# Second layer's ffn: its first four feature tiles by eight plain products instead of seven

## The chip, the cores and the metric

The kernel runs on one core of one Trainium2 chip. The metric is the device time of one execution in microseconds; runs of the same kernel differ by about 0.05%. Every number below is from one profiled execution and from the times of three more runs.

## The reference: what is computed

The kernel is one inference step of a two-layer trunk over 128 context tokens and 512 latent tokens, held side by side as 642 columns (two of them padding). Each layer is: normalise and modulate, attention, output projection and residual, normalise and modulate, a convolutional ffn and residual. The change lies in the second layer's ffn:

```python
def conv_ffn(h, w_up, conv_w, conv_b, w_down):
    u = h @ w_up                                  # 1024 -> 2 * 2816
    up = jnp.pad(u, ((0, 0), (pad, pad), (0, 0)))
    u = sum(up[:, j:j + n] * conv_w[j] for j in range(CONV_W)) + conv_b    # three taps along the tokens
    a, gt = u[..., :D_FF], u[..., D_FF:]
    return (jax.nn.silu(gt) * a) @ w_down
```

## The kernel before

Features lie on partitions and tokens along the free dimension. The ffn's 2816 features are 22 **tiles** of 128; each has an a side and a g side. The 642 columns are two **halves** of 322 and 320, and the 1024 input features two groups of four 128-row blocks (q = 0 to 3). So one tile is a 2 × 2 block product: weights A11, A12 (a side) and A21, A22 (g side) times the normalised rows B11, B21 (first half) and B12, B22 (second half).

Every matmul is done with numbers split into an upper part (a cast, `hi`) and a lower part (`lo` = number minus cast), three matmuls for each 128 × 128 block: hi·hi, hi·lo, lo·hi. A block product over four blocks q is 12 matmuls of 322 columns. A split is a cast on ScalarE (line 117) and a subtraction on VectorE or GpSimd (line 113); for weights it is made by `block`, which goes from the raw tile (`raw`, DMA of 512 KB) to a ring of ten pairs `w2`.

Seven products do for eight (Strassen's scheme in Winograd's form): with weight sums S1 to S4 (`sums`, on GpSimd) and row sums T1 to T4 (on VectorE), the products are A11·B11, A12·B21, S4·B22, A22·T4, S1·T1, S2·T2, S3·T3 (`p1` to `p7`), 84 matmuls, and `u2`, `u3`, `c22`, `c21`, `c12` add them up from PSUM on VectorE into `ca` and `cg` (line 1930). Products take PSUM tiles `p` from a ring of six, in the order in which they are made.

A tile's convolution is `gid` (ScalarE: centre tap of g into the only PSUM tile `v`), `tapg` (two VectorE steps), `silu` (ScalarE), `aid` (ScalarE: centre of a, again into `v`), `tapa`, `mul` (VectorE, into `va`), `ghi` (ScalarE cast) and `glo` (VectorE). Then four tiles at a time go through the down product (`down`), which adds to the residual `x`.

`begin` makes the second half of the attention's output projection (for each of eight column blocks j: `product`, then the residual addition `add_x` on VectorE and a square on ScalarE) and, between its blocks, the normalised first half. Its list `after` says what is issued behind each block. From line 1741 on `begin` makes tiles 0 and 1 while the second half's normalised rows and T1 to T4 come into being. `middle` makes tiles 2 and 3 (`lead`), then every tile from 4 on is one `slot` with down products of the chunk before it woven in. All engines keep the order in which the program issues; the compiler moves nothing here.

In the second half the row factor `rs1` needs the squares of all eight blocks (three small matmuls on TensorE, `rs_sum`); before the change the parts of the T sums that don't need it are made ahead of it: `scaled` and `steps` (into `second`), `shifts` (into `c1` and `first`, with the difference of shifts `ds`).

Of the kernel before, what the change touches and what calls it, by code (L numbers as in the profile page):

```python
# [1527 lines left out]
class Mix:  # L1528
# [105 lines left out]
    def begin(self, po, oT, xsrc):  # L1634
        nc, t, V, G, n, l = self.nc, self.t, self.V, self.G, range(self.KP), self.l
# [21 lines left out]
        halves = lambda tag, m: [self.T(po, tag, [P, HB], F32, m) for _ in range(m)]  # L1657
        first = [self.pair(po, "first", 4) for _ in n]
        second = [self.pair(po, "second", 4) for _ in n]
        c1, rr = halves("c1", 4), halves("rs", 3)  # L1660
        tile = lambda: self.T(po, "sq", [P, HB], F32, 3)
        ht = [[self.T(self.pm, "ht", [P, 3, HB], F32R, 8) for _ in range(2)] for _ in n]
# [41 lines left out]
        def scaled(q):  # L1704
            for v, c in self.groups(1):
                V.tensor_scalar(out=second[q][:, 0, c], in0=self.x[q][:, HB:][:, c], scalar1=mod[:, 4, q, v : v + 1], scalar2=None, op0=ALU.mult)

        def steps(q):
            for v, c in self.groups(1):
                V.scalar_tensor_tensor(out=second[q][:, 1, c], in0=self.x[q + 4][:, HB:][:, c], scalar=mod[:, 4, q + 4, v : v + 1],  # L1710
                                       in1=second[q][:, 0, c], op0=ALU.mult, op1=ALU.subtract)

        def shifts(q):
            b = first[q][:, 0]
            for v, c in self.groups(1):
                nc.scalar.activation(c1[q][:, c], b[:, c], AF.Identity, scale=-1.0, bias=mod[:, 3, q, v : v + 1])
            for v, c in self.groups(1):
                V.tensor_scalar(out=b[:, c], in0=b[:, c], scalar1=ds[:, q, v : v + 1], scalar2=None, op0=ALU.add)
# [22 lines left out]
        self.p1(0)  # L1741
        scaled(0), steps(0)
        block("S2", 0, V), block("S3", 0, V)
        self.copy1(0)
        rs1 = self.rs_of(sqs1, 1, rr[1], rr[2])
        self.p2(0), self.p1(1)
        shifts(0)
        self.copy1(1), self.copy2(0)
        self.p1(2), self.p2(1)
        qs = (3, 1, 2, 0)  # L1750

        def lows(name, q, src):
            t.low(self.rows[name, q][1], src, self.rows[name, q][0])

        def pieces(name, src, store, make, between=()):

            between, last = deque(between), None
            for q in qs:
                make(q)
                self.rows[name, q] = store(q)  # L1760
                nc.scalar.copy(self.rows[name, q][0], src(q))  # L1761
                if last is not None:
                    lows(name, last, src(last))
                if between:
                    between.popleft()()
                last = q
            lows(name, last, src(last))
            for step in between:
                step()

        row = lambda m: lambda q: [h[:, m] for h in ht[q]]
        wide = lambda q: self.act(1)
        one, two = lambda q: first[q][:, 0], lambda q: first[q][:, 1]
        three, four = lambda q: second[q][:, 0], lambda q: second[q][:, 1]

        def t2(q):
            V.tensor_mul(four(q), four(q), rs1)
            V.tensor_add(one(q), four(q), one(q))

        def t3(q):  # L1780
            for v, c in self.groups(1):
                nc.scalar.activation(four(q)[:, c], four(q)[:, c], AF.Identity, bias=ds[:, q, v : v + 1])

        def t1(q):
            V.tensor_mul(three(q), three(q), rs1)
            V.tensor_add(three(q), three(q), c1[q])

        pieces("T2", one, row(0), t2, [lambda: (self.copy2(1), self.copy1(2)), lambda: (self.p1(3), self.p2(2)),
                                       lambda: (self.copy1(3), self.copy2(2)), lambda: (self.p2(3), self.copy2(3))])
        s1 = self.T(po, "s1", [P, D])  # L1790
        self.sums(1, 0, s1)
# [36 lines left out]
    def lead(self, f, pv, nx):  # L1828
# [8 lines left out]
        if nx == self.LEAD:  # L1837
            block("A11")
# [452 lines left out]
```

## Time and profile before

| | us |
|---|---|
| three runs: median, lowest, highest | 1750.52, 1750.12, 1750.91 |
| the profiled execution: its own time, its span | 1746.39, 1744.5 |
| busy in the span: TensorE, VectorE, ScalarE, GpSimd | 1590.6, 1285.3, 928.4, 800.1 |

A busy TensorE is not one at its peak: matmuls are pipelined, and a matmul that is issued late or at the slower clock counts as busy too. Idle time of the other engines costs nothing where TensorE does not wait for them.

### The profile page before, as it was taken

What the parts mean: (1) busy time and instruction counts of PE and PEld (TensorE: products, weight loads), DVE (VectorE), ACT (ScalarE), POOL (GpSimd) and SP (SyncE); (2) the same over time, 40 slices, a digit from 0 to 9 for tenths busy, and PEclk for the clock granted to TensorE, in tenths of its full rate; (3) what the DMA queues carried; (4) which work ended last, traced back from release to release, by engine and by line L of the source; (5) the groups of instructions that cost most, each with busy time, mean ns of one, the idle gap of its engine ahead of it and who ended that gap; (6) DMA issues with size and microseconds to landing.
All of it is one profiled execution on the core that took longest, in us unless ns stands there. A gap on an engine that the chain in (4) does not pass through costs nothing.

```text
span 1744.5 us, 28162 instructions
## 1 busy us (share of the span) xinstructions
PE 1590.6 (91%) x10301; PEld 1512.9 (87%) x10301; DVE 1285.3 (74%) x2226; ACT 928.4 (53%) x1788; POOL 800.1 (46%) x769
## 2 busy tenths in 40 slices
PE   8878888888998999999988999979768999999996
PEld 2867877788898999999988999969757999999996
DVE  4895888778888779877458677774877667776765
ACT  3555777644554345534355778783444344444444
POOL 2164777462252534252171445563327456555532
PEclk9999999999999999999999999989888999999998
DMA  8440121062444444453144111114212222222311
GB/s 334 134 134 26 53 67 61 13 223 82 128 138 145 159 141 147 134 165 120 58 133 153 41 56 51 44 61 142 79 60 73 78 86 87 76 76 77 96 47 61
DMA packets 79176, 176.14 MB, mean 101 GB/s; under 512 B 11614, under 2 KB 29358, under 8 KB 79038
## 3 DMA queue, kind: packets, MB, share of 16 engines
q1 hardware_dynamic: 76542, 170.08, 30.4%
q10 hardware_dynamic: 2304, 4.20, 0.7%
q8 instruction: 81, 1.33, 0.3%
q14 instruction: 57, 0.47, 0.1%
q0 software_dynamic: 192, 0.07, 0.0%
HBM read 167.24 MB, written 8.03 MB: 100 GB/s over the span
## 4 chain that ended last, share of the span: by engine, by line
PE 55%; DVE 13%; ACT 5%; issue 4%; DMA 3%; POOL 1%; SPq 0%; DVEq 0%; ACTq 0%; POOLq 0%
PE mm L137 25%; PE p L1579 24%; DMA mraw<-in_w_mod_dram 3%; DVE acc L316 1%; PE sc L1202 1%; PE tr L1240 1%; DVE wlo L113 1%; PE o L1252 1%; DVE v L1966 1%; ACT w L117 1%; ACT whi L117 0%; DVE pt L113 0%; DVE u L505 0%; DVE nt L424 0%; DVE ha L438 0%
## 5 line engine op out<-in xcount | busy, mean ns | idle before, releaser
L314 POOL TENSOR_TENSOR acc<-acc,mt 128x512 f32<-128x512 f32 x115 | 178.7, 1554 | 262.3 <-ACT mt L313 259.4
L137 PE MATMUL mm<-ha,whi 128*128 128x352 f32 (+1 forms) x1168 | 287.3, 328 | 8.2 <-DVE u L507 3.7
L137 PE MATMUL mm<-hb,whi 128*128 128x290 f32 (+1 forms) x1168 | 245.2, 303 | 2.8 <-ACT hb L437 1.9
L137 PEld LDWEIGHTS mm<-ha,whi 128*128 128x128 f32 (+1 forms) x1168 | 202.8, 190 | 10.6 <-issue 3.8
L316 DVE SCALAR_TENSOR_TENSOR acc<-mraw,cs,acc 128x512 f32<-128x512 f32 (+1 forms) x165 | 164.9, 1006 | 53.9 <-DMA mraw<-in_w_mod_dram 50.8
L137 PEld LDWEIGHTS mm<-hb,whi 128*128 128x128 f32 (+1 forms) x1168 | 193.6, 192 | 5.3 <-issue 3.0
L137 PE MATMUL mm<-ha,wlo 128*128 128x352 f32 (+1 forms) x584 | 189.3, 324 | 0.0
L113 POOL TENSOR_TENSOR wlo<-raw,whi 128x1024 fp32r<-128x1024 f32 (+3 forms) x45 | 95.7, 2132 | 177.3 <-ACT whi L117 107.8
L137 PE MATMUL mm<-hb,wlo 128*128 128x290 f32 (+1 forms) x584 | 175.3, 300 | 0.0
L137 PE MATMUL mm<-g,whi 128*128 128x352 f32 (+1 forms) x704 | 157.5, 311 | 6.5 <-DVE x L447 5.2
L117 ACT CAST whi<-raw 128x1024 fp32r<-128x1024 f32 (+3 forms) x115 | 113.8, 995 | 69.0 <-PE mm L137 52.5
L113 POOL TENSOR_TENSOR w<-raw,w 128x512 fp32r<-128x512 f32 (+1 forms) x65 | 86.9, 1345 | 135.7 <-ACT w L117 132.3
L1579 PE MATMUL p<-g,d 128*128 128x320 f32 (+1 forms) x912 | 141.9, 314 | 4.4 <-ACT d L117 2.6
L313 ACT ACTIVATE mt<-mraw,cs 128x512 f32<-128x512 f32 x115 | 81.9, 720 | 116.6 <-DMA mraw<-in_w_mod_dram 103.7
L1579 PEld LDWEIGHTS p<-g,d 128*128 128x128 f32 x912 | 137.9, 191 | 6.4 <-ACT d L117 2.8
L1579 PE MATMUL p<-ht,w 128*128 128x322 f32 x792 | 130.6, 320 | 10.9 <-ACT ht L1761 4.8
L1579 PEld LDWEIGHTS p<-ht,w 128*128 128x128 f32 x792 | 123.8, 195 | 12.7 <-ACT ht L1761 5.4
L1579 PE MATMUL p<-hb,w 128*128 128x322 f32 (+1 forms) x696 | 115.3, 319 | 13.7 <-DVE cg L1930 7.8
L137 PEld LDWEIGHTS mm<-g,whi 128*128 128x128 f32 x704 | 118.3, 189 | 8.6 <-ACT ha L437 3.8
L1579 PEld LDWEIGHTS p<-hb,w 128*128 128x128 f32 x696 | 108.6, 196 | 15.3 <-ACT w L117 4.2
L1579 PE MATMUL p<-ha,w 128*128 128x322 f32 x696 | 113.5, 318 | 0.6 <-ACT ca L1924 0.5
L137 PEld LDWEIGHTS mm<-hb,wlo 128*128 128x128 f32 (+1 forms) x584 | 113.1, 194 | 0.2 <-issue 0.2
(339 smaller groups left out, 3835.9 us busy)
## 6 DMA issues: line engine op xcount, KB each, us to landing
raw<-in_w_up_dram SPq DMA_DIRECT2D x92, 512.0 KB, 3.6
mraw<-in_w_mod_dram SPq DMA_DIRECT2D x128, 256.0 KB, 2.9
raw<-in_w_out_dram SPq DMA_DIRECT2D x18, 512.0 KB, 4.0
raw<-in_w_in_odd_dram SPq DMA_DIRECT2D x18, 512.0 KB, 3.5
mraw<-in_w_mod_dram SPq DMA_DIRECT2D x16, 512.0 KB, 8.8
raw<-in_w_down_dram SPq DMA_DIRECT2D x16, 512.0 KB, 3.6
draw<-in_w_down_dram SPq DMA_DIRECT2D x40, 192.0 KB, 2.5
raw<-in_w_down_dram SPq DMA_DIRECT2D x16, 384.0 KB, 3.1
```

Source lines behind the costliest of these rows:

```text
L113: (engine or self.nc.vector).tensor_sub(lo, src, Fv(hi))
L117: self.nc.scalar.copy(hi, src)
L137: self.pe = self.nc.tensor.matmul(out, lhsT=l, rhs=r, start=k == 0, stop=k == n - 1)
L313: nc.scalar.activation(t, raw, AF.Copy, scale=s)
L314: nc.gpsimd.tensor_add(acc, acc, t)
L316: nc.vector.scalar_tensor_tensor(out=acc, in0=raw, scalar=s, in1=acc, op0=ALU.mult, op1=ALU.add)
L1202: nc.tensor.matmul(ps[:, c : c + n], lhsT=u.Q[:, a], rhs=x[e], start=e == 0, stop=e == 1)
L1240: nc.tensor.transpose(tp[:, j * P : (j + 1) * P], u.p[b][:, x : x + P], self.ident)
L1252: nc.tensor.matmul(u.o[:, u.t[c][2]], lhsT=v, rhs=u.t[c][e], start=c == 0 and e == 0, stop=c == 4 and e == 1)
L1579: self.t.pe = self.nc.tensor.matmul(ps[:, 0:n], lhsT=l_, rhs=r[:, 0:n], start=first and m == 0, stop=last and m == count - 1, skip_group_c ...
L1966: self.V.scalar_tensor_tensor(out=v[:, d], in0=self.flat(c)[:, s], scalar=self.t.convw[:, self.l, j, n : n + 1], in1=v[:, d], op0=ALU.mult ...
```

## The change

Tiles 0 to 3 are made by eight plain products, half by half. `plain(f, side, half)` makes both block products of one side and half into one PSUM tile (24 matmuls), and `copy` takes it to `ca` or `cg` on ScalarE. The order of TensorE is then: first halves of tiles 0, 1, 2; second halves of 2, 1, 0; tile 3, whose second half is begun with twelve matmuls of either side (products 13 and 14) and ended after its first half. I number these products 1 to 18. The second half's rows are normalised as the first half's are (`scale1`, `shift1`), and T1 to T4 (`sums_t`, `uppers`, `lowers`) are made from them during products 7 to 14, for tile 4, which is the first by seven products. Tile 0's weights are loaded and split a second time. The rings of `ca` and `cg` become 3 and 3 instead of 4 and 2.

```diff
         after = {
-            2: lambda: (self.blocks_a(0, V), self.load("a", 3), norm0(3, 4)),
-            3: lambda: (self.blocks_a(1, G), self.load("a", 0), norm0(5, 6)),
-            4: lambda: (self.blocks_a(2, G), self.load("g", 0), norm0(7), scaled(3), lower0(7), steps(3)),
-            5: lambda: (self.blocks_a(3, V), self.load("a", 1), shifts(3), scaled(1), steps(1)),
-            6: lambda: (self.sums(0, 0), shifts(1), scaled(2), steps(2)),
-            7: lambda: (self.sums(0, 1), self.load("g", 1), shifts(2)),
+            2: lambda: (self.blocks_of(0, "a", V), self.load("g", 1), norm0(3, 4)),
+            3: lambda: (self.blocks_of(0, "g", G), self.load("a", 2), norm0(5, 6)),
+            4: lambda: (self.blocks_of(1, "a", G), self.load("g", 2), norm0(7), lower0(7)),
+            5: lambda: (self.blocks_of(1, "g", G), self.load("a", 0)),
+            6: lambda: (self.blocks_of(2, "a", V), self.load("g", 0)),
+            7: lambda: None,
...
+        self.plain(0, 0, 0)
         rs1 = self.rs_of(sqs1, 1, rr[1], rr[2])
...
+        self.plain(0, 1, 0)
+        self.blocks_of(2, "g", G)
+        for k in (0, 1):
+            scale1(k), shift1(k)
+        self.copy(0, 0, 0)
+        for n, (f, side) in enumerate(((1, 0), (1, 1), (2, 0), (2, 1))):
+            self.plain(f, side, 0)
+            if n < 3:
+                for k in (2 * n + 2, 2 * n + 3):
+                    scale1(k), lower1(k - 2), shift1(k)
+            self.copy(*((0, 1), (1, 0), (1, 1), (2, 0))[n], 0)
+        lower1(6), lower1(7)
+        self.blocks_of(0, "a", G)
+
+        self.plain(2, 0, 1)
+        sums_t(0), uppers(0)
+        self.copy(2, 1, 0)
+        self.load("a", 3)
+        self.plain(2, 1, 1)
+        sums_t(1), lowers(0)
+        self.copy(2, 0, 1), uppers(1)
+        self.plain(1, 0, 1)
+        sums_t(2), lowers(1)
+        self.copy(2, 1, 1), self.gid(2), uppers(2)
+        self.blocks_of(0, "g", G), self.load("g", 3)
+        self.plain(1, 1, 1)
+        sums_t(3), self.tapg(2), lowers(2)
+        self.copy(1, 0, 1), self.silu(2), self.aid(2), uppers(3)
+        self.blocks_of(3, "g", G)
+        self.load("a", 4)
+        self.plain(0, 0, 1)
+        self.tapa(2), lowers(3)
+        self.copy(1, 1, 1)
+        self.blocks_of(3, "a", G)
+        self.load("g", 4)
+        self.plain(0, 1, 1)
+        self.copy(0, 0, 1)
+
+        self.plain(3, 1, 1, 0), self.plain(3, 0, 1, 0)
+        self.copy(0, 1, 1)
+        for q in n_:
+            upper("T1", q, source["T1"](q), self.act(1))
+            if q:
+                lower("T1", q - 1, source["T1"](q - 1))
+        lower("T1", 3, source["T1"](3))
 
     def middle(self):
+        block = lambda *names: [self.block(name, 4) for name in names]
+        tag = lambda f, *names: [getattr(self, name)(f) for name in names]
+        tag(2, "mul", "ghi")
+        self.sums(4, 0)
+        self.plain(3, 0, 0)
+        tag(1, "gid", "tapg"), tag(2, "glo"), tag(1, "silu", "aid")
+        block("A11"), self.sums(4, 1)
+        self.plain(3, 1, 0)
+        tag(1, "tapa", "mul"), block("S2")
+        tag(0, "gid"), tag(1, "ghi"), block("S3")
...
+        tag(0, "tapg"), tag(1, "glo"), tag(0, "silu", "aid"), block("S1")
...
+        tag(0, "tapa"), block("A12"), self.load("a", 5)
+        tag(0, "mul", "ghi"), block("A22")
+        self.copy(3, 1, 1), self.gid(3)
+        tag(0, "glo"), block("S4"), self.load("g", 5)
...
+    def plain(self, f, side, half, kk=None):
+        names = (("A11", "A12"), ("A21", "A22"))[side]
+        for k in (0, 1) if kk is None else (kk,):
+            key = "C", f, side, half
+            if key not in self.p:
+                self.p[key] = self.t.PS("p")
+            w = self.blocks[names[k], f]
+            row = (("B11", "B21"), ("B12", "B22"))[half][k]
+            self.matmuls(self.p[key], HB, [(self.columns(w, q), self.rows[row, q]) for q in range(self.KP)], k == 0, k == 1)
+
+    def copy(self, f, side, half):
+        c = (self.ca, self.cg)[side][f]
+        self.nc.scalar.copy(c[:, half], self.p.pop(("C", f, side, half))[:, 0:HB])
+        if half:
+            self.pads(c)
```

Three places of the order show what moves. The first is VectorE at the end of the output projection, from the residual addition of one column block (`x_2560` before, `x_2556` after) to that of the last (`x_2556` before, `x_2552` after). Before:

```order
L1590 SCALAR_TENSOR_TENSOR x_2560_13195<-p_2682_13833,mod1_83,x_2560_13195 128x190
L1590 SCALAR_TENSOR_TENSOR x_2560_13195<-p_2682_13833,mod1_83,x_2560_13195 128x128
L1601 TENSOR_TENSOR sq_2676_13812<-sq_2667_13761,sq_2676_13812 128x322
L1718 TENSOR_SCALAR first_2533_13161<-first_2533_13161,ds_2622_13523 128x190
L1718 TENSOR_SCALAR first_2533_13161<-first_2533_13161,ds_2622_13523 128x132
L1706 TENSOR_SCALAR second_2538_13166<-x_2560_13195,mod1_83 128x190
L1706 TENSOR_SCALAR second_2538_13166<-x_2560_13195,mod1_83 128x132
L1710 SCALAR_TENSOR_TENSOR second_2538_13166<-x_2587_13300,mod1_83,second_2538_13166 128x190
L1710 SCALAR_TENSOR_TENSOR second_2538_13166<-x_2587_13300,mod1_83,second_2538_13166 128x132
L1590 SCALAR_TENSOR_TENSOR x_2556_13185<-p_2685_13874,mod1_83,x_2556_13185 128x190
L1590 SCALAR_TENSOR_TENSOR x_2556_13185<-p_2685_13874,mod1_83,x_2556_13185 128x128
```

After:

```order
L1591 SCALAR_TENSOR_TENSOR x_2556_13191<-p_2677_13815,mod1_83,x_2556_13191 128x190
L1591 SCALAR_TENSOR_TENSOR x_2556_13191<-p_2677_13815,mod1_83,x_2556_13191 128x128
L1602 TENSOR_TENSOR sq_2671_13802<-sq_2662_13755,sq_2671_13802 128x322
L113 TENSOR_TENSOR w2_2680_13846<-raw_2656_13714,w2_2679_13845 128x512
L113 TENSOR_TENSOR w2_2682_13850<-raw_2656_13714,w2_2681_13849 128x512
L1591 SCALAR_TENSOR_TENSOR x_2552_13181<-p_2684_13855,mod1_83,x_2552_13181 128x190
L1591 SCALAR_TENSOR_TENSOR x_2552_13181<-p_2684_13855,mod1_83,x_2552_13181 128x128
L1617 TENSOR_TENSOR rs_2542_13170<-rs_2541_13169 128x322
```

Between the two additions stood two steps each of `shifts` (L1718), `scaled` (L1706) and `steps` (L1710); now two weight splits (tile 2's a side) stand there, and the first step of the row factor follows at once.

The second is VectorE where the lower parts of T1 (`hb`) end. Before, the last ones and what follows them:

```order
L1785 TENSOR_TENSOR second_2536_13164<-second_2536_13164,rs_2545_13173 128x322
L1786 TENSOR_TENSOR second_2536_13164<-second_2536_13164,c1_2540_13168 128x322
L113 TENSOR_TENSOR hb_2726_14182<-second_2538_13166,hb_2725_14181 128x322
L1930 TENSOR_TENSOR cg_2729_14191<-p_2720_14154,ca_2697_13978 128x322
L113 TENSOR_TENSOR hb_2728_14188<-second_2536_13164,hb_2727_14187 128x322
L113 TENSOR_TENSOR w2_2731_14195<-s1_2702_14066,w2_2730_14194 128x512
```

After:

```order
L113 TENSOR_TENSOR hb_2750_14406<-first_2532_13160,hb_2749_14405 128x322
L113 TENSOR_TENSOR hb_2752_14409<-first_2533_13161,hb_2751_14408 128x322
L113 TENSOR_TENSOR hb_2754_14413<-first_2534_13162,hb_2753_14412 128x322
L113 TENSOR_TENSOR hb_2756_14417<-first_2535_13163,hb_2755_14416 128x322
L1992 TENSOR_TENSOR va_2757_14425<-v_2734_14293,cg_2687_13885 128x642
L1969 SCALAR_TENSOR_TENSOR v_2762_14458<-cg_2689_13887,convw_434,v_2762_14458 128x641 x2
L113 TENSOR_TENSOR g_2759_14428<-va_2757_14425,g_2758_14427 128x642
L113 TENSOR_TENSOR w2_2765_14467<-raw_2739_14306,w2_2764_14466 128x512
L1969 SCALAR_TENSOR_TENSOR v_2763_14464<-ca_2688_13886,convw_434,v_2763_14464 128x641 x2
L1992 TENSOR_TENSOR va_2768_14500<-v_2763_14464,cg_2689_13887 128x642
L113 TENSOR_TENSOR w2_2770_14503<-s_2760_14430,w2_2769_14502 128x512
```

Before, additions from PSUM and a weight split follow T1, and the first convolution comes later. Now tile 2's `mul` (`va_2757`), then tile 1's taps on g (`v_2762`), tile 2's `glo`, a weight split, tile 1's taps on a (`v_2763`) and its `mul` stand behind them.

The third is ScalarE around the centre tap that follows tile 0's (after) or tile 2's (before) `ghi`, the cast into `g`. Before, with `v_2811` the centre of tile 3's g side:

```order
L1993 CAST g_2804_14558<-va_2803_14556 128x642
L117 CAST w2_2807_14574<-raw_2787_14468 128x512
L117 CAST w2_2809_14578<-s_2794_14510 128x512
L1960 ACTIVATE v_2811_14584<-cg_2799_14534,convb_436,convw_434 128x642
L117 CAST w2_2812_14587<-raw_2786_14466 128x512
L117 CAST w2_2816_14607<-raw_2787_14468 128x512
L117 CAST w2_2818_14613<-s4_2798_14531 128x512
L117 CAST w2_2824_14637<-raw_2814_14591 128x512
L1978 ACTIVATE cg_2799_14534<-v_2811_14584 128x642
```

After, with `v_2789` the centre of tile 3's g side:

```order
L1996 CAST g_2785_14565<-va_2784_14563 128x642
L117 CAST w2_2787_14568<-raw_2745_14348 128x512
L1854 COPY cg_2777_14516<-p_2747_14377 128x322
L1963 ACTIVATE v_2789_14574<-cg_2777_14516,convb_436,convw_434 128x642
L117 CAST w2_2790_14577<-s4_2766_14470 128x512
L117 CAST w2_2797_14603<-raw_2783_14561 128x512
L1981 ACTIVATE cg_2777_14516<-v_2789_14574 128x642
L1927 COPY ca_2799_14610<-p_2795_14587 128x322
```

Now a copy from PSUM, `cg_2777` from `p_2747` (product 13, closed as product 18), stands behind the `ghi` and a weight cast; before there was no copy from PSUM in this place.

## Rows read from the trace of the kernel before

**Rows 1.** Busy us by engine (instructions), granted clock (PEclk), DMA share, by stretch.
```profile
1235.80:1351.30 115.50, 81.90 (x429) 75.86 (x428) 85.07 (x148) 53.68 (x106) 52.20 (x47) 0.84 0.20 63
...
1352.00:1452.00 100.00, 99.97 (x672) 99.70 (x671) 69.59 (x118) 42.40 (x74) 53.93 (x50) 1.00 0.25 80
```

**Rows 2.** TensorE in order of time: start, us, instruction, idle before it and releaser.
```profile
1235.80 1.94 PE L1579 MATMUL p<-ha,w 128*128 128x322 f32 x12
...
1245.49 2.51 PE L359 MATMUL v<-sq,ones 128*128 128x322 f32 x4 [7.74 <-DVE sq L1601]
...
1248.66 1.44 PE L359 MATMUL v<-sq,ones 128*128 128x322 f32 x2 [0.66 <-ACT sq L1599]
...
1271.78 0.41 PE L1579 MATMUL p<-ht,w 128*128 128x322 f32 x1 [4.34 <-ACT ht L1761]
...
1328.60 3.56 PE L1579 MATMUL p<-hb,w 128*128 128x322 f32 x12 [3.92 <-DVE cg L1930]
...
1347.96 3.49 PE L1579 MATMUL p<-hb,w 128*128 128x322 f32 x12 [3.88 <-DVE cg L1930]
...
1351.28 10.91 PE L1579 MATMUL p<-g,d 128*128 128x322 f32 x72
...
1362.03 1.94 PE L1579 MATMUL p<-ha,w 128*128 128x322 f32 x12
```

**Rows 3.** VectorE and ScalarE in order of time, near the row factor.
```profile
1232.06 0.48 DVE L113 TENSOR_TENSOR ha<-first,ha 128x322 fp32r<-128x322 f32 x1
...
1241.76 2.69 DVE L1710 SCALAR_TENSOR_TENSOR second<-x,mod,second 128x190 f32<-128x190 f32 x2
...
1246.84 0.68 DVE L1710 SCALAR_TENSOR_TENSOR second<-x,mod,second 128x190 f32<-128x190 f32 x2
...
1247.43 0.67 DVE L1590 SCALAR_TENSOR_TENSOR x<-p,mod,x 128x190 f32<-128x190 f32 x2
...
1266.02 0.75 ACT L1782 ACTIVATE second<-second,ds 128x190 f32<-128x190 f32 x2
```

**Rows 4.** Groups by line, 1235 to 1352: busy us, mean ns, idle before.
```profile
L113 DVE TENSOR_TENSOR ht<-first,ht 128x322 fp32r<-128x322 f32 x8 | 3.9, 490 | 3.7 <-ACT ht L1761 3.6
...
L1761 ACT CAST hb<-second 128x322 fp32r<-128x322 f32 x8 | 3.5, 460 | 8.8 <-DVE second L1786 8.2 <-DVE second L1804 0.6
...
L1801 DVE TENSOR_TENSOR first<-first 128x322 f32<-128x322 f32 x4 | 1.9, 485 | 0.0
...
L1978 ACT ACT_TABLE_LOAD x1 | 1.3, 1283 | 1.8 <-DVE v L1966 1.8
```

**Rows 5.** Instructions on raw weights, 1150 to 1400: ns least, median, most; first and last.
```profile
L117 ACT CAST w<-raw x50: 600/614/623, 1174.1 to 1395.8; 128x512 fp32r<-128x512 f32 x50
...
L113 POOL TENSOR_TENSOR w<-raw,w x29: 1266/1300/2075, 1174.8 to 1397.2; 128x512 fp32r<-128x512 f32 x29
...
L113 DVE TENSOR_TENSOR w<-raw,w x21: 677/691/1758, 1176.6 to 1395.4; 128x512 fp32r<-128x512 f32 x21
```

**Rows 6.** One tile's convolution, in order of time (ScalarE and VectorE alone).
```profile
1308.05 0.88 ACT L1960 ACTIVATE v<-cg,convb,convw 128x642 f32<-128x642 f32 x1
...
1308.96 1.81 DVE L1966 SCALAR_TENSOR_TENSOR v<-cg,convw,v 128x641 f32<-128x641 f32 x2 [0.28 <-ACT v L1960]
...
1310.87 0.71 ACT L1978 ACTIVATE cg<-v 128x642 f32<-128x642 f32 x1 [1.94 <-DVE v L1966]
...
1311.67 0.89 ACT L1960 ACTIVATE v<-ca,convb,convw 128x642 f32<-128x642 f32 x1
...
1312.60 1.82 DVE L1966 SCALAR_TENSOR_TENSOR v<-ca,convw,v 128x641 f32<-128x641 f32 x2
...
1315.55 0.81 DVE L1989 TENSOR_TENSOR va<-v,cg 128x642 f32<-128x642 f32 x1
...
1316.39 0.73 ACT L1993 CAST g<-va 128x642 fp32r<-128x642 f32 x1 [2.04 <-DVE va L1989]
```

**Rows 7.** The page's list of transfers: count, size, median us to landing.
```profile
raw<-in_w_up_dram SPq DMA_DIRECT2D x92, 512.0 KB, 3.6
```

More of the change, by code (lines that the diff above doesn't have):

```diff
@@ L1655, in product @@
             return ps
[L1657 to L1660, printed above, removed]
+        first = [self.pair(po, "first", 4) for _ in n_]
+        second = [self.pair(po, "second", 4) for _ in n_]
+        rr = [self.T(po, "rs", [P, HB], F32, 3) for _ in range(3)]
         tile = lambda: self.T(po, "sq", [P, HB], F32, 3)
-        ht = [[self.T(self.pm, "ht", [P, 3, HB], F32R, 8) for _ in range(2)] for _ in n]
+        ht = [[self.T(self.pm, "ht", [P, 3, HB], F32R, 8) for _ in range(2)] for _ in n_]
         for j in range(3):
@@ L1709, in steps, with shift1 @@
+        def shift1(k):
+            src = second[k % 4][:, k // 4]
             for v, c in self.groups(1):
[L1710 to L1718, printed above, removed]
@@ new lines, in shift1, with upper, lower, lower1 @@
+            upper("B12" if k < self.KP else "B22", k % self.KP, src, self.act(1))
+        def upper(name, q, src, parts_):
+            self.rows[name, q] = parts_
+            nc.scalar.copy(parts_[0], src)
+        def lower(name, q, src):
+            t.low(self.rows[name, q][1], src, self.rows[name, q][0])
+        def lower1(k):
+            lower("B12" if k < self.KP else "B22", k % self.KP, second[k % 4][:, k // 4])
+        def sums_t(q):
+            b11, b21, b12, b22 = first[q][:, 0], first[q][:, 1], second[q][:, 0], second[q][:, 1]
+            V.tensor_sub(b11, b12, b11)
+            V.tensor_sub(b12, b22, b12)
+            V.tensor_sub(b22, b22, b11)
+            V.tensor_sub(b21, b21, b22)
@@ L1755, in pieces @@
[L1755 to L1791, printed above, removed]
-        pieces("T3", four, row(1), t3, [lambda: None, lambda: block("S1", 0, V), lambda: (block("A22", 0, V), self.sums(1, 2)), lambda: (block("S4", 0, V), self.sums(1, 1))])
@@ L1802, in begin @@
-        block("A22", 1)
-        self.p4(0), self.p4(1)
-        pieces("B22", four, wide, lambda q: V.tensor_add(four(q), three(q), one(q)),
-               [lambda: None, lambda: (self.c21(0), self.gid(0)), lambda: None, lambda: (self.c21(1), self.tapg(0))])
-        block("S4", 1)
-        self.silu(0), self.sums(2, 0)
-        self.p3(0)
-        self.c12(0), self.aid(0), self.sums(2, 1)
-        self.p3(1)
-        self.tapa(0), self.c12(1)
-    def middle(self):
-        self.mul(0), self.ghi(0), self.glo(0)
-        for name in ("S2", "S3", "S1", "A22", "S4"):
-            self.block(name, 2)
-        self.load("a", 3), self.load("g", 3)
-        self.gid(1)
-        for f in range(2, self.LEAD):
-            self.lead(f, f - 1, f + 1)
+        self.plain(0, 1, 0)
@@ L1871, in sums @@
             G.tensor_sub(s4, ra[:, n:], self.s[f][:, n:])
-        if part == 2 or part == 1 and tile is None and f != 1:
             G.tensor_sub(rg[:, 0:n], ra[:, 0:n], rg[:, 0:n])
@@ L1887, in block, with blocks_of @@
         self.blocks[name, f] = self.split(self.w2(), src, lo_engine or engine)
-    def blocks_a(self, f, engine):
-        self.block("A11", f, engine), self.block("A12", f, engine)
+    def blocks_of(self, f, side, engine):
+        for name in (("A11", "A12"), ("A21", "A22"))["ag".index(side)]:
+            self.block(name, f, engine)
     def product(self, name, f, row, key=None):
```

92 lines of the change are left out of this document (30 added, 62 removed).

## The prediction

> **What bounds the kernel now.** I read the table of stretches first. From 1352 on the matrix engine has work for 99.97 of 100 us at full clock; in the stretch before that, 1235.8 to 1351.3, it is busy for 81.9 of 115.5 us, at a granted clock of 0.84 [rows 1]. That stretch is the second layer's ffn from its first matmul (1235.80) to the first matmul of the down product (1351.28), and it is all that the diff touches. Its worth at full speed comes from the list of TensorE's work: 72 matmuls of the down product take 1351.28 to 1362.03, 10.75 us, or 0.1493 us each (3.58 us for 24, 1.79 for 12) [rows 2]. The stretch holds five tiles of 84 matmuls (0 to 3 and tile 4): 420, or 62.7 us. So 52.8 us are waits and slow clock. The same list names the waits: VectorE's `sq` (7.74 us, and the sums of squares that it held up end only at 1250.1), ScalarE's `ht` (4.34), VectorE's `cg` (3.92 and 3.88) [rows 2]. TensorE is bound here by operands made late, not by its own work; behind 1352 it bounds itself, so a gain in the stretch should reach the end.
>
> **What the change adds and removes.** Tiles 0 to 3 take 96 matmuls each instead of 84: 48 more, 7.2 us. The stretch then holds 468, 69.9 us, which is its floor. ScalarE, VectorE and GpSimd lose work: tiles 0 to 3 needed 28 weight splits and now 20 (16, and tile 0's four a second time); GpSimd's 16 weight sums for them go; so do VectorE's 20 additions from PSUM, for 8 more copies on ScalarE (0.46 us each by the cast of the same size [rows 4]). Two more 512 KB loads meet DMA engines that are 20% busy [rows 1] and are asked for a dozen microseconds before use; I cost them at nothing, and a load that were not early enough would show 3.6 us [rows 7].
>
> **The walk.** Engines take instructions in order, so I follow the new order with durations from rows, from VectorE's step at 1232.06 [rows 3]; up to it the two orders differ by an 8-column subtraction on VectorE and by which weights are split.
>
> (a) To the second product. Before, TensorE waits at the sums of squares because the last residual addition stands on VectorE behind the `second`/`first` steps and runs at 1247.43 [rows 3], although its matmuls ended by 1235.8. These steps are gone. VectorE ends its last common step at 1232.5; then stand, up to that addition, one `ha` piece (0.49), two additions (0.67), two adds of squares (0.48, as any sum of that size) and two weight splits (0.69): 4.2 us [rows 3 to 5]. GpSimd makes four splits at 1.3 us in the same time; I take three of them, 3.9 us, as time in which they hold VectorE (bounds: none, and 5.2), and the last addition stands near 1240.6. With 0.67, a square (0.46, as a cast of its size) and the last sum (0.72, half of the 1.44 at the slow clock [rows 2]) product 2 starts at 1242.5, against 1250.1 for the same point before.
>
> (b) Products 2 to 12, 264 matmuls: 39.4 us, to 1281.9. Their second halves begin at 1260.4 and need the eight normalised rows. The row factor takes six steps of this size, 2.9 us at 0.49, and one or two of GpSimd's splits hold it: 5 us, an estimate. VectorE's first pair of halves takes 0.68, then ScalarE spends 0.75 + 0.46 us on each row [rows 3, 4], 9.7 us, and 1.4 on three copies: 1259.3. It is covered by 1.1 us; whatever that cover lacks is lost at once.
>
> (c) Tile 3's first twelve matmuls of either side, to E, the end of product 14. VectorE works from 1259.3 through four groups of four subtractions and two groups of three lower parts ahead of the first tap: 16 × 0.485 + 6 × 0.49 = 10.7 us [rows 4], and with the four splits of GpSimd that fall there, 1.3 us each [rows 5], it is at 1275.2. The taps take 1.8 [rows 6]; then on ScalarE the table load 1.28, silu 0.71, the centre 0.89, three casts 1.38, two weight casts 1.22: 1282.5 [rows 4 to 6]. GpSimd's lower parts of tile 3 follow from the first cast on (1281.9), three until A11 is complete, 3.9, with a VectorE step of 0.49 let in before two of them: 1286.8. The last ten matmuls of product 14 take 1.5: E = 1288.3. By matmuls alone it would be 1285.5.
>
> (d) E to the product S3·T3 of tile 4. There is one `v` tile in PSUM, so convolutions go one behind the other: from centre to the next tile's centre 0.91 + 1.91 + 0.80 + 0.93 + the taps 1.8 and the product, 7.2 us [rows 6]. Tile 2's product now stands on VectorE behind the lower parts of T1, which wait for E: +1.1, product +0.83, ScalarE's cast +0.65, then tiles 1 and 0 (14.4, and A12's split of 0.69 in between) bring tile 0's product to its end at E + 17.7. ScalarE's order then is `ghi(0)` (0.73), A22's cast (0.61), and only behind them the copy (0.46) of tile 3's last product, whose PSUM tile S3·T3 takes: E + 19.5, and 1 us for splits that hold VectorE (bounds: none, and 4). That is 1308.8. TensorE has 72 + 24 matmuls, 14.3 us, in this time, and stands for 6.
>
> (e) To the down product. After such a pause twelve matmuls take 3.3 us (1347.96 to 1351.28 [rows 2]); three products 5.4; then S4·B22 waits for `c22(4)`, which stands behind tile 3's convolution and the next tile's S2 step: 2.5 (before it was 3.88 at this place); itself 1.8. Sum 13.0: the down product starts at 1321.8 instead of 1351.28, **29.5 us earlier**. In the profiled execution, 1744.5 of span in 1746.39, the time becomes 1716.9; that execution lies 4.1 us under the median of the runs, 1750.52, so the median becomes **1721.0**.
>
> **A rule weighed.** The rows show that a VectorE split takes 0.69 us as a rule and 1.76 at most [rows 5], and that a pair of halves took 2.69 us where 0.68 is usual [rows 3]: waits of about one GpSimd split. The Trainium skill, "SBUF — State Buffer", section "SBUF: two separate sides", says that a VectorE instruction with two SBUF inputs and a GpSimd instruction that reads SBUF exclude each other for a whole instruction. The trace agrees as far as these numbers go. By the rule GpSimd's splits add in series, as (a) and (c) count them; without it E falls to its 1285.5 and the median to about 1718.2.
>
> **Rivals.** *PE-bound* (0.18): nothing in the new order is late, convolutions hide. Three sums (2.1) and 69.9 us from 1235.80: down product at 1307.8, 43.5 us gained, 1707 at the extreme and up to 1715. For it: GpSimd and VectorE lose work. Against: the chain of (d) has no slack for two whole convolutions after E. *The chain is longer* (0.19): before, one convolution went from 1308.05 to 1316.39 undisturbed [rows 6], but elsewhere VectorE's other work stands between its steps; at 2.5 us more for each of three, and 5 more in (c) where VectorE, ScalarE and GpSimd hand over in turn, 12.5 us go back: 1733.5, with a range of 1728 to 1740. *Given back later* (0.04): the rest runs at the rate of transfers or splits, so an earlier start only queues there: 1750. Against it is 99.97 of 100 us busy, with DMA engines at a quarter [rows 1]. *Slower* (0.04): one mechanism, exclusion on VectorE between 1243 and E. There stand 16 half rows, 16 subtractions and 24 lower parts with two SBUF operands: 5.4 + 7.8 + 11.8 = 25 us. Were each held as the worst split was (1.758 over 0.691, 2.54 [rows 5]), 38.5 us would be added: 9 slower, 1759.5. It decides from a factor of 2.3 on; the median of 0.691 against the least, 0.677, speaks against it.
>
> **How the numbers follow.** The walk has 0.55, with a range of its own of 1715 to 1728 (E at 1285.5 to 1292, 1 to 3 us more or less in (d) and (e)). PE-bound 0.18, longer 0.19, given back 0.04, slower 0.04. The range to hold eight in ten reaches into both neighbours: 1709 to 1735. A measurement can tell about 0.2%, 3.5 us, from no change; faster by more than that is all of the first three cases, 0.92; same 0.04, slower 0.04.
>
> **What would show it.** Right: TensorE's sums of squares held up by VectorE and ScalarE for about 2 us and not 7.7; the matrix engine without a gap over 1 us from 1243 to 1282; one gap of some 6 us, ended by ScalarE's copy of `cg`, in tile 4; granted clock near 1 between 1243 and 1299; the down product near 1322. Wrong: a gap at the first product of the second half (normalised rows late), a longer one at tile 3's twelve matmuls, ended by GpSimd's `w`, or an idle matrix engine behind the down product. The forecast fails most easily in (d), where one tile's convolution more or less behind E is 7 us.

## The result, and the profile after

| | before | after |
|---|---|---|
| median of the runs, lowest to highest, us | 1750.32, 1746.03 to 1750.91 | 1722.87, 1717.81 to 1723.75 |
| profiled execution: time, span | 1746.39, 1744.5 | 1723.75, 1721.7 |
| product 1 to the down product (distance) | 115.48 | 90.71 |
| down product to the end of the span | 393.2 | 394.7 |

The ratio is 0.9842 [0.9817, 0.9867], and the medians in the table differ by 27.5 us. The two profiled executions differ by less, 22.8 us of span, because the one of before is the second lowest of its runs and the one of after the highest. What is steadier is a distance inside one execution: from the start of product 1 to the start of the down product it fell from 1351.28 − 1235.80 = 115.48 us [rows 2] to 1327.04 − 1236.33 = 90.71, by **24.8 us**; the prediction had 86.0, a gain of 29.5.

The first fence is the table of stretches: length, busy us (instructions) of TensorE, its weight loads, VectorE, ScalarE and GpSimd, granted clock, DMA share, GB/s. It answers [rows 1]: TensorE now stands or runs slowly for less, at a clock of 0.94 instead of 0.84, and what comes behind is nearly as dense as before.

```profile
1236.33:1327.04 90.71, 75.30 (x477) 72.23 (x475) 68.57 (x106) 52.53 (x109) 34.13 (x33) 0.94 0.20 67
1328.00:1428.00 100.00, 99.50 (x668) 98.97 (x667) 71.41 (x117) 43.34 (x75) 55.30 (x52) 1.00 0.26 82
```

TensorE in order of time, after (answers [rows 2]):

```profile
1236.33 3.74 PE L1580 MATMUL p<-ha,w 128*128 128x322 f32 x24
1239.91 1.25 PE L359 MATMUL v<-sq,ones 128*128 128x322 f32 x4
1242.37 0.81 PE L359 MATMUL v<-sq,ones 128*128 128x322 f32 x2 [1.22 <-ACT sq L1600]
1242.78 18.29 PE L1580 MATMUL p<-ha,w 128*128 128x322 f32 x120
1260.90 25.11 PE L1580 MATMUL p<-hb,w 128*128 128x322 f32 x168
1285.85 7.33 PE L1580 MATMUL p<-ha,w 128*128 128x322 f32 x48
...
1305.95 2.16 PE L1580 MATMUL p<-hb,w 128*128 128x322 f32 x12 [0.17 <-ACT cg L1854]
1318.39 3.59 PE L1580 MATMUL p<-ha,w 128*128 128x322 f32 x12 [10.28 <-ACT ca L1927]
...
1325.15 2.05 PE L1580 MATMUL p<-hb,w 128*128 128x322 f32 x12 [1.33 <-DVE cg L1933]
1327.04 10.91 PE L1580 MATMUL p<-g,d 128*128 128x322 f32 x72
```

The 7.74 us at the sums of squares are 1.22; products 2 to 14 (120 + 168 matmuls) run without a gap, and E, the end of product 14, is 1285.85. Four waits of 0.2 to 1.1 us between 1297 and 1304 are left out. One large wait remains: A12·B21 of tile 4 (12 matmuls from 1318.39) stands 10.28 us for ScalarE's `copy1(4)`. The next fence follows that wait back, VectorE, ScalarE and GpSimd in order of time:

```profile
1284.56 1.32 POOL L1869 TENSOR_TENSOR s<-raw 128x512 f32<-128x512 f32 x1 [0.71 <-DMA raw<-in_w_up_dram]
1285.07 5.68 DVE L113 TENSOR_TENSOR hb<-first,hb 128x322 fp32r<-128x322 f32 x4 [3.68 <-ACT hb L1715]
...
1288.85 1.56 POOL L1874 TENSOR_TENSOR raw<-raw,raw 128x512 f32<-128x512 f32 x1
1290.68 0.81 DVE L1992 TENSOR_TENSOR va<-v,cg 128x642 f32<-128x642 f32 x1
...
1299.70 0.83 DVE L1992 TENSOR_TENSOR va<-v,cg 128x642 f32<-128x642 f32 x1
...
1305.48 0.42 ACT L1854 COPY cg<-p 128x322 f32<-128x322 f32 x1
...
1308.53 0.82 DVE L1992 TENSOR_TENSOR va<-v,cg 128x642 f32<-128x642 f32 x1
...
1310.54 0.42 ACT L1854 COPY cg<-p 128x322 f32<-128x322 f32 x1
1310.71 1.38 POOL L113 TENSOR_TENSOR w<-raw,w 128x512 fp32r<-128x512 f32 x1 [4.33 <-ACT w L117]
1312.04 0.10 POOL L1936 MEMSET cg<- 128x2 f32 x1
1312.17 0.89 ACT L1963 ACTIVATE v<-cg,convb,convw 128x642 f32<-128x642 f32 x1 [1.21 <-POOL cg L1936]
...
1314.15 1.34 DVE L113 TENSOR_TENSOR w<-raw,w 128x512 fp32r<-128x512 f32 x1 [3.17 <-ACT w L117]
...
1315.41 1.81 DVE L1969 SCALAR_TENSOR_TENSOR v<-cg,convw,v 128x641 f32<-128x641 f32 x2
...
1317.31 0.71 ACT L1981 ACTIVATE cg<-v 128x642 f32<-128x642 f32 x1 [3.19 <-DVE v L1969]
1317.91 0.42 ACT L1927 COPY ca<-p 128x322 f32<-128x322 f32 x1
...
1324.61 0.48 DVE L1933 TENSOR_TENSOR cg<-p,cg 128x322 f32<-128x322 f32 x1
```

Read from below (1305.48, the copy of product 16, is needed further on): `copy1(4)` (1317.91) only needs a product that TensorE ended near 1299.6, but stands in ScalarE's order behind `silu(3)` (1317.31). That waits for `tapg(3)` (1315.41), which stands on VectorE behind A11's lower part of tile 5 (1314.15). `gid(3)` (1312.17) waited for the padding of `cg` on GpSimd, which stands there behind A22's split; and all of it follows the products (L1992) of tiles 2, 1 and 0, 1290.68, 1299.70 and 1308.53, about 9 us apart. The first of these stands behind T1's four lower parts, which took 5.68 us because GpSimd made tile 4's four weight sums at the same time.

### The profile page after: what moved, and what is told of

It reads as the page before. It is cut to its first block, busy times and chain, and to the rows that moved or that the text cites. A ratio compares the mean times of both kernels' runs of the same rounds, so it can differ in the third digit from the quotient of the medians.

```text
span 1721.7 us, 28186 instructions
## 1 busy us (share of the span) xinstructions
PE 1586.1 (92%) x10349; PEld 1512.6 (88%) x10349; DVE 1272.2 (74%) x2181; ACT 927.6 (54%) x1792; POOL 783.6 (46%) x757
## 3 DMA queue, kind: packets, MB, share of 16 engines
q8 instruction: 81, 1.33, 0.3%
## 4 chain that ended last, share of the span: by engine, by line
PE 53%; DVE 14%; ACT 6%; issue 4%; DMA 3%; POOL 2%; SPq 0%; DVEq 0%; ACTq 0%; POOLq 0%
PE mm L137 24%; PE p L1580 22%; DMA mraw<-in_w_mod_dram 2%; DVE acc L316 1%; PE sc L1202 1%; PE tr L1240 1%; DVE wlo L113 1%; PE o L1252 1%; DVE nt L424 1%; DVE v L1969 1%; DVE ha L438 1%; ACT whi L117 1%; POOL acc L314 0%; DVE pt L113 0%; DVE x L447 0%
## 5 line engine op out<-in xcount | busy, mean ns | idle before, releaser
L113 POOL TENSOR_TENSOR w<-raw,w 128x512 fp32r<-128x512 f32 (+1 forms) x72 | 96.4, 1349 | 151.4 <-ACT w L117 141.2
L1580 PE MATMUL p<-ha,w 128*128 128x322 f32 x792 | 126.6, 314 | 11.0 <-ACT ca L1927 10.3
L1580 PEld LDWEIGHTS p<-ha,w 128*128 128x128 f32 x792 | 120.9, 191 | 12.0 <-ACT ca L1927 10.6
L1580 PE MATMUL p<-hb,w 128*128 128x322 f32 (+1 forms) x792 | 124.0, 310 | 1.5 <-DVE cg L1933 1.3
L1580 PEld LDWEIGHTS p<-hb,w 128*128 128x128 f32 x792 | 118.5, 189 | 2.3 <-DVE cg L1933 1.6
L137 PEld LDWEIGHTS mm<-ha,wlo 128*128 128x128 f32 (+1 forms) x584 | 110.6, 189 | 0.4
```

Source lines behind the costliest of these rows:

```text
L113: (engine or self.nc.vector).tensor_sub(lo, src, Fv(hi))
L137: self.pe = self.nc.tensor.matmul(out, lhsT=l, rhs=r, start=k == 0, stop=k == n - 1)
L1580: self.t.pe = self.nc.tensor.matmul(ps[:, 0:n], lhsT=l_, rhs=r[:, 0:n], start=first and m == 0, stop=last and m == count - 1, skip_group_c ...
```

## The experiments

All distances are from the start of product 1; with it each profile is compared at its own zero. The changed kernel, run again beside the first experiments:

> The changed kernel once more, beside the next three on one chip. The same as its first runs: 1717.8 to 1723.8 us, ratio to the kernel before 0.982 to 0.987. In its profile the matrix engine should again stand about 10 us at A12 x B21 of tile 4, with the down product near 1327 us and E near 1286.

1725.65 us (1717.64 to 1728.10), ratio 0.9852 [0.9827, 0.9877]; distance 90.95, the wait 10.30 us. The median lies 1.9 us above the band expected; the distance repeats to 0.24 us.

**The copy first.**

```diff
         self.p1(f)
+        if f == self.PLAIN:
+            self.copy1(f)
         sums(0), block("A11"), conv("tapg", "silu")
-        self.copy1(f)
+        if f > self.PLAIN:
+            self.copy1(f)
```

> The copy of tile 4's product 1 stands ahead of silu(3) on ScalarE instead of behind it; nothing else is moved. Theory: the 10.3 us wait at A12 x B21 is that copy's, so A12 x B21 starts near 1314 instead of 1318.4. But the chain of convolutions sets the end: c22(4) still stands on VectorE behind tile 3's convolution, at 1324.6, and the 4 us come back as a longer wait at S4 x B22, possibly with the slow clock there (3.4 us for twelve instead of 1.8). Down product 1326.5 to 1328.5, time within 2 us of the changed kernel. Rival (a wait is worth its length): down product near 1323, 4 us faster. Rival (the wait was not this copy's): A12 x B21 stays at 1318.

1727.19 us, ratio 0.9873 [0.9850, 0.9895]; down product at 92.67, 1.7 to 2.0 us later than without the edit and 0.5 beyond the theory's band (1328.5 is 92.2 behind product 1). TensorE's rows, with product 1 at 1239.97:

```profile
1318.02 3.59 PE L1580 MATMUL p<-ha,w 128*128 128x322 f32 x12 [5.87 <-ACT ca L1927]
...
1329.26 3.56 PE L1580 MATMUL p<-hb,w 128*128 128x322 f32 x12 [5.46 <-DVE cg L1933]
1332.64 7.62 PE L1580 MATMUL p<-g,d 128*128 128x322 f32 x50
```

The wait at A12·B21 is 4.4 us shorter, so it was this copy's, and it all comes back at S4·B22, which waits 5.46 us for `c22(4)` on VectorE. Its twelve matmuls take 3.4 us to the down product, at a granted clock of 0.50, instead of 1.9 at 1.00: the engine that got work earlier only stood twice. The longest wait was not worth its length, nor anything.

**Tile 1's convolution early.** Tile 2's product and tile 1's convolution stand ahead of T1's pieces (`mul` with `True` writes over `cg`).

```diff
         self.copy(0, 1, 1)
+        self.mul(2, True), self.gid(1), self.tapg(1), self.silu(1), self.aid(1), self.tapa(1), self.mul(1, True)
         for q in n_:
             upper("T1", q, source["T1"](q), self.act(1))
...
-        tag(2, "mul", "ghi")
+        tag(2, "ghi")
...
-        tag(1, "gid", "tapg"), tag(2, "glo"), tag(1, "silu", "aid")
+        tag(2, "glo")
...
-        tag(1, "tapa", "mul"), block("S2")
+        block("S2")
```

> Tile 2's product of the two sides and the whole convolution of tile 1 stand ahead of the upper and lower parts of T1 on VectorE and ScalarE, and these two products are written in place, over cg. Theory (the chain of convolutions sets the down product): the product of tile 2 falls to 1281.5 instead of 1290.7, that of tile 1 to about 1288.7 instead of 1299.7, that of tile 0 to about 1299.5 instead of 1308.5; gid(3) follows near 1303 instead of 1312.2, and the down product starts 9 us earlier, near 1318; time 1712 to 1716, ratio to the kernel before about 0.979. Rival (the lower parts of T1 are needed as soon): S1 x T1 of tile 4 waits for VectorE instead, and the gain is under 3 us.

1716.64 us, ratio 0.9809 [0.9785, 0.9834], against 0.9852 for the changed kernel on the same chip; once more, beside the last experiment:

> The kernel with tile 1's convolution early, once more beside the next one on one chip: 1712 to 1717 us, and 83 us from product 1 to the down product.

1715.58 us, ratio 0.9812 [0.9785, 0.9838]. Distances 82.76 and 82.77: 8.0 to 8.2 us earlier, expected 9. The rows are TensorE's in the first of the two, whose product 1 starts at 1231.51:

```profile
1305.57 3.58 PE L1580 MATMUL p<-ha,w 128*128 128x322 f32 x12 [6.57 <-ACT ca L1928]
...
1314.27 10.86 PE L1580 MATMUL p<-g,d 128*128 128x322 f32 x72
```

So the chain of convolutions sets the down product. T1's lower parts, needed only by S1·T1, which starts 15 us after they end, had been put ahead of it; moved behind, they don't make S1·T1 wait. There they take 1.71 us, since they start when GpSimd's weight sums are nearly over; so this edit also removes the collision that the next one takes away alone, and the two shares of the 8 us are not separated here.

**No weight sums beside T1.** In `middle`, for tile 4:

```diff
-        self.sums(4, 0)
+        self.s[4], self.s4[4] = self.raw["a", 4], self.raw["a", 4][:, 0 : self.B]
...
-        block("A11"), self.sums(4, 1)
+        block("A11")
```

> GpSimd's four weight sums of tile 4 are left out; its blocks S1 to S4 are split from the raw weights instead, so tile 4's seven products are not those of the method. Nothing else is changed. Theory (the sums stretch T1's four lower parts from 2.0 to 5.7 us, and the chain of convolutions stands behind these): the lower parts take 2 us again, the product of tile 2 stands at 1287.1 instead of 1290.7, and the down product starts 3.6 us earlier, 1323.4; time 1716.5 to 1720 where the changed kernel has 1721 to 1723. Rival (the lower parts are slow for another reason, such as their two F32 operands): they stay at 1.4 us each, and the down product at 1327.

1723.16 us, ratio 0.9846 [0.9820, 0.9872], which is not told apart from 0.9852, and the time lies above the 1716.5 to 1720 expected (the changed kernel beside it, 1725.65, lay above its own band too); but the distance is 87.41, 3.3 to 3.5 us less, where 3.6 was expected. VectorE's row:

```profile
1286.15 1.79 DVE L113 TENSOR_TENSOR hb<-first,hb 128x322 fp32r<-128x322 f32 x4 [3.68 <-ACT hb L1715]
```

The four lower parts take 1.79 us without GpSimd's sums beside them, 5.68 with them. The Trainium skill, "SBUF — State Buffer", section "SBUF: two separate sides", says that a VectorE instruction with two SBUF inputs, as these are, and a GpSimd instruction that reads SBUF exclude each other for a whole instruction; the trace agrees: 3.89 us more, nearly the length of three of GpSimd's sums of 1.3 to 1.6 us.

**The front alone**, in the kernel before:

```diff
-            4: lambda: (self.blocks_a(2, G), self.load("g", 0), norm0(7), scaled(3), lower0(7), steps(3)),
+            4: lambda: (self.blocks_a(2, G), self.load("g", 0), norm0(7), lower0(7)),
...
         self.p1(0)
+        for q in (3, 1, 2):
+            scaled(q), steps(q), shifts(q)
         scaled(0), steps(0)
```

(and likewise without them in the next three entries of the list).

> The kernel before, with seven products for tiles 0 to 3, and one thing changed: the steps on second and first for three of the four pairs of rows (scaled, steps, shifts) stand behind the last residual addition on VectorE instead of ahead of it. Theory (the change's first 7.8 us come only because the plain products need neither these steps nor the row factor): the sums of squares are ready about 7 us earlier after product 1, but the T rows need the moved steps, and the wait for ht of 4.3 us grows by what was won; down product 0 to 2 us earlier, time 1746 to 1752. Rival (taking the steps off the way of the last addition is the gain, whatever the products): down product 7 us earlier, time near 1743.

1745.65 us, ratio 0.9986 [0.9972, 1.0000]; distance 113.40 instead of 115.48. TensorE, with product 1 at 1238.21:

```profile
1242.77 3.33 PE L359 MATMUL v<-sq,ones 128*128 128x322 f32 x6 [2.62 <-DVE sq L1601]
1247.66 9.19 PE L1579 MATMUL p<-ha,w 128*128 128x322 f32 x60 [1.56 <-ACT ca L1926]
1259.24 5.37 PE L1579 MATMUL p<-ha,w 128*128 128x322 f32 x24 [2.40 <-ACT ca L1926]
...
1270.73 0.64 PE L1579 MATMUL p<-ht,w 128*128 128x322 f32 x1 [4.34 <-ACT ht L1763]
...
1283.05 5.20 PE L1579 MATMUL p<-hb,w 128*128 128x322 f32 x23 [0.30 <-DVE hb L113]
...
1351.61 10.63 PE L1579 MATMUL p<-g,d 128*128 128x322 f32 x70
```

The sums of squares start 4.6 us behind product 1 instead of 9.7, and 2.1 us of these 5.1 arrive. Time and distance lie just past the theory's bounds (1746 us, 2 us), and the distance is far from the rival's 7 us. The place was not the theory's: `ht` still waits 4.34 us. At the end of that wait 3.5 us are left, since ScalarE's copies, waited for 1.56 and 2.40 us, come late: the second stands behind a cast of `ht` that waits for VectorE. Most of the rest goes where 23 matmuls of T1's rows take 5.20 us; before, they take 3.69. So with seven products most of the gain at the front is given back; whether it is with plain products too, the next experiment asks.

**The front's work put back**, in the changed kernel, behind blocks 4, 5 and 6 of the list:

```diff
+        def again(q):
+            for n in range(4):
+                for v, c in self.groups(1):
+                    V.tensor_scalar(out=second[q][:, n % 2, c], in0=self.x[q][:, HB:][:, c], scalar1=mod[:, 4, q, v : v + 1], scalar2=None, op0=ALU.mult)
...
```

> The changed kernel, with VectorE work put back ahead of the last residual addition: 24 scalings of the second half's rows in the place of the former steps, whose results are overwritten unread. Theory (behind the second product the matrix engine has no slack up to the wait in tile 4, and the chain of convolutions starts from the same place): whatever the sums of squares are late by (4 to 8 us after product 1, against 6.45 us of distance now) comes out at the down product in full, within 1 us; distance from product 1 to the down product 95 to 99 us instead of 90.7. Rival (the 10 us wait in tile 4 takes it up): 91 to 92 us.

1726.96 us, ratio 0.9879 [0.9858, 0.9900]; distance 97.75. Product 2 starts 12.68 us behind product 1 instead of 6.45, 6.2 later, and the down product 6.8 to 7.0 later. TensorE, product 1 at 1236.49:

```profile
1249.17 19.75 PE L1580 MATMUL p<-ha,w 128*128 128x322 f32 x120
...
1325.59 3.59 PE L1580 MATMUL p<-ha,w 128*128 128x322 f32 x12 [10.29 <-ACT ca L1932]
...
1334.24 10.91 PE L1580 MATMUL p<-g,d 128*128 128x322 f32 x72
```

The 120 matmuls behind the pause take 19.75 us instead of 18.29, and the wait in tile 4 is as long as it was (10.29): it doesn't take anything up, since the chain that ends it starts from the same products. The gain of term (a) counts in full.

**The short chain.** Beside tile 1's convolution, the rest of the order in `middle` and in tile 4's slot:

```diff
-        tag(0, "mul", "ghi"), block("A22")
-        self.copy(3, 1, 1), self.gid(3)
+        self.copy(3, 1, 1)
+        tag(0, "mul"), self.gid(3), tag(0, "ghi"), block("A22")
...
+        if f == self.PLAIN:
+            self.copy1(f), conv("tapg", "silu"), sums(0)
+            self.p6(f), self.p7(f), self.p5(f)
+            self.u2(f), self.u3(f), self.c22(f)
+            sums(1), conv("aid", "tapa")
+            self.parts_d(*downs[0]), self.load_d(*downs[2])
+            conv("mul", "ghi", "glo")
+            block("A11", "S2", "S3", "S1")
...
```

> The kernel with tile 1's convolution early, and further: tile 3's gid stands right behind tile 0's product, the copy of tile 4's product 1 ahead of silu(3), u2, u3 and c22 of tile 4 ahead of tile 3's second taps, and the next tile's four weight blocks behind these. Theory (only the order of the hand-overs between VectorE and ScalarE keeps the matrix engine waiting in tile 4): it stands for less than 2 us in all from the ffn's first matmul to the down product, the clock stays up, and the distance from product 1 to the down product falls from 82.8 to 73 to 76 us; time 1706 to 1710. Rival (the next tile's weights, now made later, become the wait): the down product starts as early, but the matrix engine stands behind it at the first products of tile 5, and the time stays above 1712.

1715.97 us, ratio 0.9818 [0.9797, 0.9839]. TensorE, product 1 at 1238.26:

```profile
1306.35 2.06 PE L1580 MATMUL p<-ha,w 128*128 128x322 f32 x12 [0.56 <-ACT ca L1928]
...
1311.80 0.45 PE L1580 MATMUL p<-g,d 128*128 128x322 f32 x2
...
1325.61 0.56 PE L1580 MATMUL p<-g,d 128*128 128x322 f32 x2 [2.87 <-ACT d L117]
...
1331.51 1.95 PE L1580 MATMUL p<-ha,w 128*128 128x322 f32 x12
```

The down product starts at 73.54, as the theory had it, and the wait at A12·B21, 6.57 us in the kernel with tile 1's convolution early, is 0.56. But its 72 matmuls take 19.7 us instead of 10.7, with seven pauses of 5.7 us in all, the longest (2.87) for a weight of its own, and slower matmuls behind them; and tile 5 starts at 93.25, where the kernel with tile 1's convolution early has 93.46: of the 9.2 us won, 9.0 are given back, as the rival had it in kind, though mainly at the down product's own weights and not at tile 5's. On ScalarE the cast that ends the longest pause stands behind the centre tap of tile 4's a side.

**The next tile too.** `p2`, `copy2`, `p4`, `c21`, `gid(4)`, `p3` and `c12` stand ahead of tile 5's seven blocks, with the second down product's weights between them, and:

```diff
+                if half == 0 and f == self.PLAIN and n == 0:
+                    self.parts_d(*downs[2])
                 if half == 0:
                     for name in steps[n] if n < 2 else ():
                         getattr(self, name)(f)
...
```

> The short chain once more, with what stood in the way behind it moved too: tile 4's c21, c12 and gid stand on VectorE and ScalarE ahead of the seven weight blocks of tile 5, and the weights of the second and third down product are made ahead of tile 4's convolution. Theory (in the short chain the gain was given back at the down product, whose weights stand on ScalarE behind tile 4's convolution): the 72 matmuls of the down product run with less than 2 us of pauses, and the first product of tile 5 starts 85 to 89 us behind product 1, where the short chain has 93.25 and the kernel with tile 1's convolution early 93.46; time 1706 to 1712. Rival (tile 5's weights are too late now): the first products of tile 5 wait for them, 91 us or more, time 1714 to 1718.

1712.55 us, ratio 0.9792 [0.9766, 0.9818], the lowest median of all; tile 5 starts at 91.30, 2.2 us earlier than in the kernel beside it and not the 4.5 to 8.5 expected. TensorE, product 1 at 1236.17:

```profile
1322.59 5.04 PE L1580 MATMUL p<-g,d 128*128 128x322 f32 x22 [2.42 <-DVE d L113]
1327.47 1.94 PE L1580 MATMUL p<-ha,w 128*128 128x322 f32 x12
```

VectorE's rows, three of the four splits for tile 5:

```profile
1316.77 3.49 DVE L113 TENSOR_TENSOR w<-s,w 128x512 fp32r<-128x512 f32 x2
...
1320.19 1.74 DVE L113 TENSOR_TENSOR w<-raw,w 128x512 fp32r<-128x512 f32 x1
```

The pauses in the down product still sum to over 4 us (five, of 0.19 to 2.42), more than the 2 expected. The last is for the third weight tile's split on VectorE, which I put behind four splits for tile 5. These took 6.6 us where four splits take 2.8 as a rule (0.69 each [rows 5]), with GpSimd's splits at the same time, as T1's lower parts did beside its sums; this was not tried alone. The theory's size fell. The rival's number, 91 us or more, came out, but not its cause: the first product of tile 5 follows the down product without a wait. The time lies between the two bands, and as the intervals overlap, only the distance tells this kernel from the one beside it.

## Why the prediction was right, and where it was off

The mechanism was right and the median within 1.9 us, but the gain of the stretch was 4.7 us too large, and two errors of opposite sign stand behind that: E came 3.0 us earlier than forecast, the down product 7.7 us later behind E. That the median lies closer than the distance is luck: run again, the changed kernel had a median of 1725.65, 2.8 us higher.

*(a)* held: product 2 starts 6.45 us behind product 1, predicted 6.7; the last residual addition starts 4.8 us behind it, as predicted. That the sum of (a) fits so well is luck too: where it has 3.9 us for GpSimd's splits, VectorE's rows have two places that take about 1 us longer than usual, beside GpSimd's splits, and two waits for ScalarE's casts, 1.26 and 1.07 us, which the prediction didn't count:

```profile
1234.33 1.49 DVE L113 TENSOR_TENSOR ha<-first,ha 128x322 fp32r<-128x322 f32 x1 [1.26 <-ACT ha L1689]
...
1238.86 2.37 DVE L113 TENSOR_TENSOR w<-raw,w 128x512 fp32r<-128x512 f32 x2 [1.07 <-ACT w L117]
```

The two front experiments show that this gain arrives in full here and for the smaller part in the old order. *(b)* held: products 2 to 12 without a gap, at a granted clock of 1.00, second halves from 1260.90. One detail was wrong without a price: the change makes two weight loads fewer, not two more; the page counts 90 of them now, 92 before [rows 7].

*(c)* was over-sized. E lies 49.5 us behind product 1, predicted 52.5. Of four GpSimd splits that I put ahead of tile 2's first tap only two fell there (1259.80, 2.86 us for both); VectorE's row for the tap, predicted at 1275.2:

```profile
1271.33 1.81 DVE L1969 SCALAR_TENSOR_TENSOR v<-cg,convw,v 128x641 f32<-128x641 f32 x2
```

The hand-over behind it was early enough, and E is that of matmuls alone. That is the number of "without the rule", but not because the rule is wrong: the other splits came later and met VectorE where it had time, as its idle 3.68 us ahead of T1's lower parts show.

*(d)* is the step that failed. From E to the down product 33.5 us were predicted, and 41.2 measured. The single stop, ended by ScalarE late in tile 4, was there, but longer (10.28 us, not 6), at another product (A12·B21, not S3·T3) and ended by another copy. S3·T3 had not waited for the copy of tile 3's last product, as I put it: it had ended by 1305.8, and that copy came at 1310.54. Counted off in the order in which products are made, as said above, the six PSUM tiles give that copy. But S1·T1 (1305.95) waited for the copy of product 16 (1305.48), so here they came back in the order of their copies; S3·T3 then had the tile of product 15, which is worked out from that order and not shown by a wait. Three things were mis-sized or missing: tile 2's product at E + 4.8 instead of E + 1.1, since I gave T1's lower parts no collision with GpSimd's sums (the experiment without sums gives 3.3 to 3.5 us back); the two convolutions behind it, 17.85 us from product to product instead of 15.7 (14.4, a cast and a split); and, missing altogether, half of tile 3's convolution with tile 5's first split, 1310.54 to 1317.91, which ScalarE's order puts ahead of `copy1(4)`. I had followed the chain to the copy that I expected, and not ScalarE's list to its end.

*(e)* was right in kind: twelve matmuls behind the pause take 3.4 us (predicted 3.3), at a granted clock of 0.50, and S4·B22 waits for `c22(4)`, 1.33 us (predicted 2.5). Three products instead of five were left behind the later wait, 8.65 us instead of 13.0, which hid part of (d).

*Rivals.* PE-bound falls: the distance is 90.7 us where matmuls alone give 72.0. The longer chain holds in kind for the convolutions (9.0 and 8.8 us from product to product where (d) counts 7.2, so about 1.7 more and not 2.5) and not for (c), where it put 5 us; its 1728 to 1740 us is not reached. Given back later falls for the change itself (394.7 us behind the down product's start, before 393.2); but something like it, with another cause, came true for my own next step, the short chain. Slower by exclusion falls: products 2 to 14 never wait.

## To carry to other kernels

A wait's releaser is the last name of a chain: before pricing the wait, follow every engine's list up to the releasing instruction, since what stands in front of it in order counts as much as what it needs. Taking away the longest wait alone gained nothing here; putting one convolution ahead, into time in which VectorE stood idle and out of GpSimd's way, gained 8 us. And where runs scatter by some us, compare distances between two events of the same execution: they repeated to 0.24 us where medians differed by 3.

## Not expected of the hardware

The code ahead of product 1 is the same in the changed kernel and in the one with tile 1's convolution early, and yet product 1 started 1231.51 us into the span in one execution and 1241.44 in another. The first three runs of before had differed by 0.05%; eleven runs beside the first experiments spread from 1744.82 to 1757.23, 0.7%. Much of the scatter arises early. The fences show the same two places in TensorE's order, in the kernel with tile 1's convolution early (product 1 at 1231.51) and then in the changed kernel run again (1241.44):

```profile
399.51 1.89 PE L337 MATMUL b<-mred,sel 128*128 128x16 f32 x8 [5.70 <-DVE mred L326]
...
562.80 0.43 PE L137 MATMUL mm<-g,whi 128*128 128x352 f32 x1 [0.43 <-DVE g L113]
```

```profile
402.31 1.89 PE L337 MATMUL b<-mred,sel 128*128 128x16 f32 x8 [5.88 <-DVE mred L326]
...
571.06 0.43 PE L137 MATMUL mm<-g,whi 128*128 128x352 f32 x1 [0.44 <-DVE g L113]
```

The second is 2.8 us behind at the first place, 8.3 at the second and 9.9 at product 1. Between the two places both did the same work at nearly the same granted clock (0.99 and 0.98, from 444 to 563 us and from 447 to 571); in the second TensorE stood for VectorE's `u` three times, 5.0 us in all, in the first once, 2.2 us. What held VectorE up was not tried and stays open.
